# The product with the norm's weights at the end of the feed-forward layers, on GpSimd

## The chip, the cores and the metric

The program runs on one core of one Trainium2 chip. The metric is the device time of one execution in microseconds (us). The engines are PE (matmuls and transposes), VectorE (DVE in the rows), ScalarE (ACT), GpSimd (POOL) and SyncE (SP, whose queue starts most transfers). Each engine takes its instructions in a fixed order and waits at its head until what the instruction needs is there.

## What is computed

Two blocks, one after the other, on 512 rows of 1024 numbers. The first has two layers of attention and of a mixture of experts. The second has two layers, each with a feed-forward part, a mixer and a second feed-forward part. All four feed-forward parts end in the same way, and that ending is what the change touches:

```python
def rms_norm_2(x, gain):
    x32 = x.astype(jnp.float32)
    y = x32 * lax.rsqrt(jnp.mean(x32 * x32, axis=-1, keepdims=True) + RMS_EPS) * gain.astype(jnp.float32)
    return y.astype(x.dtype)

def swiglu(h, w_gate, w_up, w_down):
    return (jax.nn.silu(h @ w_gate) * (h @ w_up)) @ w_down

f = swiglu(rms_norm_2(h, g[0]), ffn_w_gate[layer, 0], ffn_w_up[layer, 0], ffn_w_down[layer, 0])
h = h + 0.5 * rms_norm_2(f, g[1])
hm = rms_norm_2(h, g[2])
```

So at the end of a feed-forward part each row of its result f is multiplied by the norm's weights (g[1], with the 0.5 in it) and by one number, the reciprocal root of its mean square, and added to h. The next stage begins with another such norm of the new h.

## The kernel before

The 512 rows are four tiles t of 128 rows; h lies in `X` and f in `F`, both 128 partitions by 4 tiles by 1024 columns, float32, in SBUF. A tile is worked on in two halves of 512 columns. Matmuls in float32 precision are made of three passes (`mm3`, lines 207 to 209): each operand is split into a rounded high part (ScalarE, line 202) and the rest (line 203, VectorE, now and then GpSimd).

`ffn` goes over the 2816 hidden columns in three groups c. For the last, c = 2, `tok_major` runs the last four weight rows tile by tile: 24 matmuls of 512 columns finish a tile, 12 for a half. Then, for tile t, `evac` adds the two banks to `F` (line 1113) and calls `post_add`:

- `rms(hs, "post")`: ScalarE squares each half and sums it up (line 1043; the tile named `junk` takes the squares, `ss` the sums), VectorE joins the two sums to `ms` (line 1045), GpSimd raises it to the power -0.5, `rr` (line 1047).
- line 1060 multiplies each half of `F` by the weights `gain`, in place.
- line 1062 adds `F` times `rr` to each half of `X`.
- `feed` (line 241 and 222) makes the norm for the next stage: the same four steps over `X`, `xn` as the normed tile on VectorE in two halves, four transposes on PE for each half, and the split of the transposed columns to `xt` (ScalarE line 202, VectorE line 203). PE needs `xt` of all four tiles for the next stage's first matmuls, or of tiles 0 and 1 for their first halves.

At the last feed-forward part there is no `feed`: each half of `X` is sent to the output.

The order on each engine is made by a scheduler from the code and a model of durations; `issue_after(after)` keeps line 1060, on the engine of the instruction named `after`, behind the tile's second addition (line 1113). It adds nothing for an instruction on another engine. Line 1060 has other callers too (the mixers' ends), which pass no `after`.

Of the kernel before, what the change touches and what calls it, by code (L numbers as in the profile page):

```python
# [14 lines left out]
OP = mybir.AluOpType  # L15
# [94 lines left out]
class Core:  # L110
# [942 lines left out]
    def post_add(self, t, hs, g, feed=True, after=None):  # L1053

        V = self.nc.vector
        r = self.rms(hs, "post")
        xs = self.halves(self.X[:, t, :])
        with self.tc.issue_after(after) if after else nullcontext():
            for h in range(2):
                V.tensor_tensor(hs[h], hs[h], g[:, h * 512:(h + 1) * 512], op=OP.mult)  # L1060
        for h in range(2):
            V.scalar_tensor_tensor(xs[h], hs[h], r, xs[h], op0=OP.mult, op1=OP.add)  # L1062
        if self.nxt and feed:
            self.feed(t)
        if not self.nxt:
            o = self.out[0, t * P:(t + 1) * P, :]
            for q, y, x in zip((self.nc.sync, self.nc.scalar), self.halves(o), xs):
                q.dma_start(y, x)
# [423 lines left out]
```

## Time and profile before

| | us |
|---|---|
| median of 3 runs | 2849.36 |
| lowest and highest | 2843.97, 2851.26 |
| the profiled execution | 2851.15 |
| its span in the profile | 2849.4 |

Busy in the profiled execution: PE 2754.2 us, VectorE 1525.3, ScalarE 1194.9, GpSimd 233.9. The clock granted to PE is at its full level in nearly all of the span (0.983 on average). A busy PE is one whose pipeline is not empty; what it loses is seen in the rows on whom it waited for. In the timeline a row's bracket is the idle time of the engine ahead of it, and what ended it.

The rows that the prediction rests on stand below, behind the change.

### The profile page before, as it was taken

To read this page: it belongs to the slowest core of one execution; us is meant where nothing else is said; L and a number is where in the kernel's file an instruction comes from. 1 tells how busy PE (TensorE), PEld (TensorE's weight loads), DVE (VectorE), ACT (ScalarE), POOL (GpSimd) and SP (SyncE) were. 2 spreads that over 40 slices of the span, in tenths; PEclk is the share of its full clock that TensorE was granted. 3 is DMA by queue.
4 is the path that set the end of the run, shared out by engine and by line. 5 is a ranking of instruction groups with operands and counts; after the bars stand their busy time and mean duration, and the time that the engine had idled before them with its cause. 6 is when DMAs were issued, how large, how long until landed. Compare 5 with 4: busy or idle time off the path is not lost.

```text
span 2849.4 us, 35986 instructions
## 1 busy us (share of the span) xinstructions
PE 2754.2 (97%) x14092; PEld 2278.2 (80%) x14092; DVE 1525.3 (54%) x2819; ACT 1194.9 (42%) x2141; POOL 233.9 (8%) x233
## 2 busy tenths in 40 slices
PE   8998999998999999999999999999999999999998
PEld 6766986766896888888888887998888787788886
DVE  7965987976896323356533237343233644632334
ACT  4374983375893222234423224232322445532222
POOL 0031211041211000010100001000000000100000
PEclk9999999999999999999999999999999999999999
DMA  4316976216995323314232333333232314133320
GB/s 168 79 41 223 341 290 215 60 35 219 318 342 186 107 89 104 104 57 136 92 100 89 103 103 109 133 122 104 89 104 89 111 39 141 53 105 103 97 92 33
DMA packets 180000, 365.07 MB, mean 128 GB/s; under 512 B 14544, under 2 KB 115152, under 8 KB 172272
## 3 DMA queue, kind: packets, MB, share of 16 engines
q1 hardware_dynamic: 169264, 336.35, 35.2%
q0 software_dynamic: 9984, 25.31, 2.6%
q8 instruction: 112, 1.84, 0.3%
q10 hardware_dynamic: 576, 1.05, 0.1%
q14 instruction: 64, 0.52, 0.1%
HBM read 343.73 MB, written 27.33 MB: 130 GB/s over the span
## 4 chain that ended last, share of the span: by engine, by line
PE 74%; DVE 6%; ACT 1%; issue 1%; POOL 1%; DMA 1%; POOLq 0%; DVEq 0%; ACTq 0%; SPq 0%
PE psa L209 19%; PE psa L207 19%; PE psa L208 19%; PE pst L209 3%; PE pst L207 3%; PE pst L208 3%; PE psa L1297 1%; PE pst L1325 1%; DVE xn L241 1%; DVE hl L203 1%; POOL rr L1047 1%; DVE X L1062 1%; PE pst L222 1%; PE pst L1315 0%; DVE xt L203 0%
## 5 line engine op out<-in xcount | busy, mean ns | idle before, releaser
L203 DVE TENSOR_TENSOR hl<-raw,hl 128x1024 fp32r<-128x1024 f32 (+2 forms) x451 | 552.3, 1231 | 778.6 <-ACT hl L202 777.6
L202 ACT CAST hl<-raw 128x1024 fp32r<-128x1024 f32 (+1 forms) x456 | 471.8, 1042 | 682.2 <-PE psa L209 327.9
L209 PE MATMUL psa<-xt,hl 128*128 128x512 f32 (+1 forms) x1632 | 602.7, 369 | 1.9 <-DVE hl L203 1.9
L207 PE MATMUL psa<-xt,hl 128*128 128x512 f32 (+1 forms) x1632 | 603.0, 370 | 0.7 <-ACT xt L202 0.7
L208 PE MATMUL psa<-xt,hl 128*128 128x512 f32 (+1 forms) x1632 | 603.0, 370 | 0.2 <-DVE xt L203 0.2
L209 PEld LDWEIGHTS psa<-xt,hl 128*128 128x128 f32 x1632 | 309.0, 189 | 53.2 <-DVE hl L203 2.3
L207 PEld LDWEIGHTS psa<-xt,hl 128*128 128x128 f32 x1632 | 309.0, 190 | 52.8 <-ACT xt L202 1.1
L208 PEld LDWEIGHTS psa<-xt,hl 128*128 128x128 f32 x1632 | 309.1, 189 | 51.8 <-DVE xt L203 0.6
L207 PE MATMUL psa<-hl,xt 128*128 128x512 f32 (+2 forms) x608 | 245.4, 405 | 3.5 <-ACT hl L202 3.5
L209 PE MATMUL psa<-hl,xt 128*128 128x512 f32 (+2 forms) x608 | 245.5, 404 | 0.0
L208 PE MATMUL psa<-hl,xt 128*128 128x512 f32 (+2 forms) x608 | 241.8, 398 | 3.2 <-DVE hl L203 3.0
L1098 ACT ACTIVATE silu<-psa 128x512 f32<-128x512 f32 x88 | 52.6, 597 | 345.7 <-PE psa L209 345.7
L207 PE MATMUL psa<-hl,hT 128*128 128x512 f32 (+1 forms) x480 | 189.0, 394 | 0.0
L209 PE MATMUL psa<-hl,hT 128*128 128x512 f32 (+1 forms) x480 | 187.8, 391 | 0.0
L208 PE MATMUL psa<-hl,hT 128*128 128x512 f32 (+1 forms) x480 | 187.8, 391 | 0.0
L1099 DVE TENSOR_TENSOR silu<-silu,psa 128x512 f32<-128x512 f32 x88 | 60.5, 687 | 217.5 <-PE psa L209 217.1
L1047 POOL TENSOR_TENSOR rr<-ms,consts 128x1 f32<-128x1 f32 x52 | 38.6, 744 | 1632.4 <-DVE ms L1045 1621.5
L207 PEld LDWEIGHTS psa<-hl,xt 128*128 128x128 f32 x608 | 139.2, 229 | 21.7 <-ACT hl L202 3.7
L208 PEld LDWEIGHTS psa<-hl,xt 128*128 128x128 f32 x608 | 139.6, 230 | 18.8 <-DVE hl L203 5.3
L209 PEld LDWEIGHTS psa<-hl,xt 128*128 128x128 f32 x608 | 139.3, 229 | 13.5 <-issue 1.0
L207 PE MATMUL psa<-hl,xgT 128*96 128x256 f32 x512 | 145.5, 284 | 0.5 <-ACT xgT L202 0.5
L208 PE MATMUL psa<-hl,xgT 128*96 128x256 f32 x512 | 143.1, 280 | 0.0
(366 smaller groups left out, 4419.2 us busy)
## 6 DMA issues: line engine op xcount, KB each, us to landing
raw<-in_ffn_w_gate_dram SPq DMA_DIRECT2D x44, 1024.0 KB
raw<-in_ffn_w_up_dram SPq DMA_DIRECT2D x44, 1024.0 KB
raw<-in_ffn_w_down_dram SPq DMA_DIRECT2D x44, 1024.0 KB
raw<-in_w_up_dram SPq DMA_DIRECT2D x16, 1024.0 KB
raw<-in_w_gate_dram SPq DMA_DIRECT2D x12, 1024.0 KB
raw<-in_w_down_dram SPq DMA_DIRECT2D x12, 1024.0 KB
xt<-in_w_down_dram SPq DMA_DIRECT2D x12, 1024.0 KB
xt<-in_w_gate_dram SPq DMA_DIRECT2D x10, 1024.0 KB
```

Of the source, the lines that this page charges most:

```text
L202: self.nc.scalar.copy(hi, src)
L203: return (self.nc.gpsimd if pool else self.nc.vector).tensor_tensor(lo, src, hi.bitcast(F32), op=OP.subtract)
L207: mm(out, lhs[0], rhs[0], start=start, stop=False)
L208: mm(out, lhs[0], rhs[1], start=False, stop=False)
L209: mm(out, lhs[1], rhs[0], start=False, stop=stop)
L222: self.nc.tensor.transpose(ps[:, k * P:(k + 1) * P], src[:, (4 * h + k) * P:(4 * h + k + 1) * P], self.ident)
L241: self.nc.vector.scalar_tensor_tensor(o, i, r, gh, op0=OP.mult, op1=OP.mult)
L1047: nc.gpsimd.tensor_tensor(r, ms, self.c("nhalf")[:, :1], op=OP.pow)
L1062: V.scalar_tensor_tensor(xs[h], hs[h], r, xs[h], op0=OP.mult, op1=OP.add)
L1098: A.activation(s, acc[0], AF.Silu)
L1099: V.tensor_tensor(s, s, acc[1], op=OP.mult)
L1297: PE.matmul(ps[:, (j - j0) * nk + b * P:(j - j0) * nk + (b + 1) * P], qT[half(par), j, :], kv["k", g, kb][half(par), j, :], start=True, st ...
```

## The change

One line of `post_add` is changed. Where `after` is given, which only the feed-forward parts do, the product of line 1060 is issued on GpSimd, else on VectorE as before. There are 4 parts, 4 tiles and 2 halves: 32 instructions of 128x512.

```diff
         with self.tc.issue_after(after) if after else nullcontext():
             for h in range(2):
-                V.tensor_tensor(hs[h], hs[h], g[:, h * 512:(h + 1) * 512], op=OP.mult)
+                (self.nc.gpsimd if after else V).tensor_tensor(hs[h], hs[h], g[:, h * 512:(h + 1) * 512], op=OP.mult)
```

Since the product writes the half that ScalarE's square reads, it waits for that square. The scheduler lays all engines' orders out anew around it.

GpSimd at the end of the first feed-forward part, before; the pairs of `rr` are those of `F` and of `X` of one tile, and `hl` is the rest of a weight split for the next stage:

```order
L1047 TENSOR_TENSOR rr_11585<-ms_11583,consts_72 128x1
L1047 TENSOR_TENSOR rr_11597<-ms_11595,consts_72 128x1
L1047 TENSOR_TENSOR rr_11648<-ms_11646,consts_72 128x1
L1047 TENSOR_TENSOR rr_11660<-ms_11658,consts_72 128x1
L1047 TENSOR_TENSOR rr_11711<-ms_11709,consts_72 128x1
L203 TENSOR_TENSOR hl_11831<-raw_11823,hl_11831 128x1024
L1047 TENSOR_TENSOR rr_11723<-ms_11721,consts_72 128x1
L1047 TENSOR_TENSOR rr_11774<-ms_11772,consts_72 128x1
L1047 TENSOR_TENSOR rr_11786<-ms_11784,consts_72 128x1
```

The same place in the change:

```order
L1060 TENSOR_TENSOR F_9482<-F_9482,gain_9479 128x512 x2
L1047 TENSOR_TENSOR rr_11585<-ms_11583,consts_72 128x1
L1047 TENSOR_TENSOR rr_11597<-ms_11595,consts_72 128x1
L1060 TENSOR_TENSOR F_9482<-F_9482,gain_9479 128x512 x2
L1047 TENSOR_TENSOR rr_11648<-ms_11646,consts_72 128x1
L1047 TENSOR_TENSOR rr_11660<-ms_11658,consts_72 128x1
L1060 TENSOR_TENSOR F_9482<-F_9482,gain_9479 128x512 x2
L1047 TENSOR_TENSOR rr_11711<-ms_11709,consts_72 128x1
L1060 TENSOR_TENSOR F_9482<-F_9482,gain_9479 128x512
L1047 TENSOR_TENSOR rr_11723<-ms_11721,consts_72 128x1
L203 TENSOR_TENSOR hl_11831<-raw_11823,hl_11831 128x1024
L1060 TENSOR_TENSOR F_9482<-F_9482,gain_9479 128x512
```

Both products of a tile stand ahead of its first `rr`, the next tile's behind its second; the last tile's first product stands ahead of tile 2's second `rr`, the other behind the weight split. At the ends of the second and third part the order is the same but for the split, which isn't there.

VectorE at the same end, from the additions of tile 0 on, before:

```order
L1113 TENSOR_TENSOR F_9482<-F_9482,psa_11478 128x512
L1113 TENSOR_TENSOR F_9482<-F_9482,pst_11482 128x512
L1060 TENSOR_TENSOR F_9482<-F_9482,gain_9479 128x512
L1045 TENSOR_SCALAR ms_11583<-ss2_11579 128x1
L1060 TENSOR_TENSOR F_9482<-F_9482,gain_9479 128x512
L1062 SCALAR_TENSOR_TENSOR X_6608<-F_9482,rr_11585,X_6608 128x512 x2
L1113 TENSOR_TENSOR F_9482<-F_9482,psa_11486 128x512
L1045 TENSOR_SCALAR ms_11595<-ss2_11591 128x1
L241 SCALAR_TENSOR_TENSOR xn_11599<-X_6608,rr_11597,gain_11471 128x512 x2
L1113 TENSOR_TENSOR F_9482<-F_9482,pst_11490 128x512
```

And in the change:

```order
L1113 TENSOR_TENSOR F_9482<-F_9482,psa_11478 128x512
L1113 TENSOR_TENSOR F_9482<-F_9482,pst_11482 128x512
L1045 TENSOR_SCALAR ms_11583<-ss2_11579 128x1
L1062 SCALAR_TENSOR_TENSOR X_6608<-F_9482,rr_11585,X_6608 128x512 x2
L1113 TENSOR_TENSOR F_9482<-F_9482,psa_11486 128x512
L1045 TENSOR_SCALAR ms_11595<-ss2_11591 128x1
L241 SCALAR_TENSOR_TENSOR xn_11599<-X_6608,rr_11597,gain_11471 128x512 x2
L1113 TENSOR_TENSOR F_9482<-F_9482,pst_11490 128x512
```

Only the products are gone here; the second addition of the next tile still stands behind both halves of `xn`.

PE at the transposes (line 222) of tile 1 of the same end, before; `psa` and `pst` are banks, and the lines 207 to 209 are matmuls of the last tile:

```order
L208 MATMUL psa_11502<-hl_11542,hT_11336 128x512
L209 MATMUL psa_11502<-hl_11542,hT_11336 128x512
L207 MATMUL psa_11502<-hl_11547,hT_11402 128x512
L222 MATMUL pst_11665<-consts_72,xn_11662 128x128 x4
L208 MATMUL psa_11502<-hl_11547,hT_11402 128x512
L222 MATMUL psa_11672<-consts_72,xn_11662 128x128 x4
L209 MATMUL psa_11502<-hl_11547,hT_11402 128x512
```

In the change:

```order
L208 MATMUL pst_11498<-hl_11550,hT_11464 128x512
L209 MATMUL pst_11498<-hl_11550,hT_11464 128x512
L207 MATMUL psa_11502<-hl_11539,hT_11274 128x512
L222 MATMUL pst_11665<-consts_72,xn_11662 128x128 x4
L222 MATMUL psa_11672<-consts_72,xn_11662 128x128 x4
L208 MATMUL psa_11502<-hl_11539,hT_11274 128x512
L209 MATMUL psa_11502<-hl_11539,hT_11274 128x512
```

Both groups stand earlier in the last tile's matmuls, and no matmul is left between them.

## Rows read from the trace of the kernel before

**Rows 1.** The page, part 1: busy us, share of the span, instructions
```profile
PE 2754.2 (97%) x14092; PEld 2278.2 (80%) x14092; DVE 1525.3 (54%) x2819; ACT 1194.9 (42%) x2141; POOL 233.9 (8%) x233
```

**Rows 2.** PE's waits at ends 1, 2, 3: us in total, times, longest
```profile
PE pst L222 <- DVE xn L241: 2.8, 3, 1.2
PE psa L209 <- DVE hl L203: 0.5, 1, 0.5
...
PE pst L222 <- DVE xn L241: 1.8, 3, 1.2
...
PE psa L208 <- DVE hl L203: 2.2, 1, 2.2
PE pst L222 <- DVE xn L241: 1.5, 2, 1.2
```

**Rows 3.** Timeline, end 1, tile 0: start, us, engine, line, instruction [idle before <-releaser]
```profile
1246.36 0.69 DVE L1113 TENSOR_TENSOR F<-F,pst 128x512 f32<-128x512 f32 x1 [2.03 <-PE pst L209]
...
1247.14 0.63 ACT L1043 ACTIVATE junk<-F 128x512 bf16<-128x512 f32 x1 [2.06 <-DVE F L1113]
...
1247.90 0.21 DVE L1045 TENSOR_SCALAR ms<-ss 128x1 f32<-128x1 f32 x1 [0.25 <-ACT junk L1043]
...
1248.03 0.68 DVE L1060 TENSOR_TENSOR F<-F,gain 128x512 f32<-128x512 f32 x1
1248.19 0.93 POOL L1047 TENSOR_TENSOR rr<-ms,consts 128x1 f32<-128x1 f32 x1 [338.79 <-DVE ms L1045]
...
1249.15 1.42 DVE L1062 SCALAR_TENSOR_TENSOR X<-F,rr,X 128x512 f32<-128x512 f32 x2 [0.44 <-POOL rr L1047]
...
1250.69 0.63 ACT L1043 ACTIVATE junk<-X 128x512 bf16<-128x512 f32 x1
...
1251.81 0.55 POOL L1047 TENSOR_TENSOR rr<-ms,consts 128x1 f32<-128x1 f32 x1 [2.69 <-DVE ms L1045]
...
1252.39 1.42 DVE L241 SCALAR_TENSOR_TENSOR xn<-X,rr,gain 128x512 f32<-128x512 f32 x2 [0.73 <-POOL rr L1047]
...
1253.20 0.66 PE L222 MATMUL pst<-consts,xn 128*128 128x128 f32 x4 [1.21 <-DVE xn L241]
```

**Rows 4.** Timeline of PE, end 1: transposes of tiles 0 to 2
```profile
1253.93 0.60 PE L222 MATMUL psa<-consts,xn 128*128 128x128 f32 x4
...
1260.99 0.66 PE L222 MATMUL pst<-consts,xn 128*128 128x128 f32 x4
1261.73 0.60 PE L222 MATMUL psa<-consts,xn 128*128 128x128 f32 x4
...
1271.54 0.66 PE L222 MATMUL pst<-consts,xn 128*128 128x128 f32 x4 [1.18 <-DVE xn L241]
```

**Rows 5.** Products on GpSimd (ns min/median/max; mean ns), weight cast on ScalarE
```profile
L587 POOL TENSOR_TENSOR X<-X,gb x6: 2362/2384/2408, 240.9 to 684.5; 128x1024 f32<-128x1024 f32 x6
...
L529 POOL TENSOR_TENSOR rows<-rows,den 128x512 f32<-128x512 f32 x8 | 8.2, 1038 | 110.9 <-DVE den L527 110.2 <-DVE m L516 0.7
...
L202 ACT CAST hl<-raw 128x1024 fp32r<-128x1024 f32 (+1 forms) x456 | 471.8, 1042 | 682.2 <-PE psa L209 327.9
```

**Rows 6.** Timeline: VectorE and GpSimd at the same time, near 1377 and 452 us
```profile
1377.29 3.52 DVE L241 SCALAR_TENSOR_TENSOR xn<-X,rr,gain 128x512 f32<-128x512 f32 x2
...
1377.73 2.53 POOL L203 TENSOR_TENSOR hl<-raw,hl 128x1024 fp32r<-128x1024 f32 x1
...
451.87 0.68 DVE L203 TENSOR_TENSOR xt<-psa,xt 128x512 fp32r<-128x512 f32 x1
...
451.43 2.36 POOL L587 TENSOR_TENSOR X<-X,gb 128x1024 f32<-128x1024 f32 x1 [3.07 <-DVE X L586]
```

**Rows 7.** Timeline, last end, tile 3
```profile
2838.67 0.19 ACT L1043 ACTIVATION_READ_ACCUMULATOR junk<-F 128x1 f32 x1
...
2839.24 0.86 POOL L1047 TENSOR_TENSOR rr<-ms,consts 128x1 f32<-128x1 f32 x1 [4.58 <-DVE ms L1045]
2840.14 1.42 DVE L1062 SCALAR_TENSOR_TENSOR X<-F,rr,X 128x512 f32<-128x512 f32 x2 [0.44 <-POOL rr L1047]
```

## The prediction

> **What bounds the kernel now.** I read the page's busy shares first: PE is busy 97% of the span, VectorE 54% [rows 1]. PE takes its instructions in a fixed order, so a wait of PE at its head goes into the time in full, and a microsecond saved on VectorE is worth something only where PE waits for VectorE. So next I read whom PE waits for around the three feed-forward ends that have a stage behind them (from 1236, 1726 and 2236 us; I call them ends 1, 2, 3), and the fourth end, at 2836 us, with which the program stops. At end 1 PE waits 2.8 us for `xn` and 0.5 for a weight split, at end 2 1.8 for `xn`, at end 3 1.5 for `xn` and 2.2 for a weight split, 8.8 us in all [rows 2]. That is the most that a faster ending could bring.
>
> Then I read one tile's chain from the timeline [rows 3], start to start. Second half of F added 1246.36, its square on ScalarE 1247.14 (0.78 later), `ms` 1247.90 (0.76), `rr` on GpSimd 1248.19, X updated 1249.15, second square of X 1250.69 (1.54), the next `rr` 1251.81 (1.12), `xn` 1252.39 (0.58), transposes on PE 1253.20 (0.81), for which PE has waited 1.21. VectorE's second product with the weights runs from 1248.03 inside the wait for `rr`; it only lengthens `rr` from 0.55 to 0.93.
>
> **What the change does to one tile.** It removes 32 products of 0.68 us from VectorE, eight at each end, and puts 32 on GpSimd. The product writes the half that the square reads, so it can't run beside that square; it starts when the square is done. In GpSimd's printed order both products of a tile stand ahead of that tile's `rr`, and behind the second `rr` of a tile stands the next tile's first product (two, where its squares are done).
>
> *Price of one product on GpSimd.* No row shows it. The same form at twice the width takes 2.36 to 2.41 us; a product with a broadcast operand at this width 1.04 [rows 5]. Half of 2.385 is 1.19, and I add 0.09 for the start-up, which doesn't halve: 1.28. The ends are 1.04 and 1.4; I stay by the first row, since the form is the same. The Trainium skill (GPSIMD Engine Reference, section 3.1, Elementwise) gives 4497 ns for 2048 columns with two inputs, which would be an estimate of 1.12 for this width; by it the sum below falls by about 3.5 us. No run here shows that figure.
>
> *First cost: the product is now ahead of `rr`.* Square's start to its end 0.73, hand-over 0.08, product 1.28, `rr` to X 0.58. The chain from the addition to the transposes is then 0.78 + 0.81 + 1.28 + 0.58 + 1.54 + 1.12 + 0.58 + 0.81 = 7.50 us, against 6.84 in the trace [rows 3].
>
> *Second cost: the two engines shut each other out.* At 1377 us a pair of `xn` took 3.52 us instead of 1.42, while GpSimd worked from 1377.73 to 1380.26 on a split with two SBUF inputs: the second half waited for it and was done 0.55 after it. A VectorE instruction with one operand in PSUM ran its usual 0.68 in the middle of a GpSimd product [rows 6]. Now GpSimd has a product queued directly behind the `rr` that releases `xn`, so it stands between the two halves of `xn`: the second half ends about 1.13 + 0.55 = 1.7 us after the first, not 0.67. The addition of the next tile is queued behind that half on VectorE, so the whole next chain starts later too.
>
> *Third cost: PE's order.* The transposes stand earlier among the matmuls than before: the first by one, the second tile's by five (24 matmuls between the first tile's and the second's, counted in the printed order, where there were 29), with its two groups back to back. Matmul slots are 0.23: 7.06 us between 1253.93 and 1260.99 for one group of transposes and 29 matmuls [rows 4].
>
> **The sum.** Waits of PE at end 1, group by group. Tile 0, first half: 1.21 + 0.64 (the longer chain) + 0.23 (one place earlier) = 2.1; second half 1.2 (1.7 less its own 0.35 and a matmul). Tile 1: the next chain starts 0.15 before the transposes of tile 0's second half, so 7.50 - 0.15 = 7.35 lies between them; PE has work for 7.06 - 5 x 0.23 = 5.9, so it waits 1.4, then 1.7 - 0.35 = 1.4 for the second half. Tile 2: three more things stand in that chain: a copy of 512 transposed columns ahead of the square (0.5, half of the cast of 1024), a weight cast of 1.04 between the squares of X [rows 5], and the last tile's first product ahead of `rr` (1.25): 10.2 us from group to group. Before, 9.81 lay between them [rows 4], of which 1.7 was waiting [rows 2, 4], so some 8.1 of work; 0.2 to 0.8 less now, and I take 7.7: a wait of 2.5. Its second half waits 2.3 at end 1, where a weight split is next on GpSimd, such a one as the 2.53 of rows 6. Tile 3 at end 1: GpSimd still has that split, the last product and `rr` to do, X follows some 5.3 us after tile 2's `xn`, and `xn` some 10.1 after it; PE, with 44 half-width matmuls in between, is there after 9.3: 1.6 and 0.6. Sum of end 1: 2.1 + 1.2 + 1.4 + 1.4 + 2.5 + 2.3 + 1.6 + 0.6 = 13.1. At ends 2 and 3 GpSimd has a product and no split behind tile 2's `rr` (1.2, not 2.3), and tile 3's transposes stand behind 29 full matmuls, so that 0.8 and 0.3 are left for it: 10.6 and 10.1. Walking the old order in the same way gave 1.2, 0.2, 0.8, 1.3 and 0.6 at end 1, where the trace has 1.21, none, 0.5, 1.18 and 0.4 (what is left of the 2.8) [rows 2 to 4], which is why I trust the steps to half a microsecond each.
>
> Less what is there now [rows 2]: 13.1 - 3.3 = 9.8, 10.6 - 1.8 = 8.8, 10.1 - 3.7 = 6.4; at end 3 the 2.2 for the weight split goes, because its cast and split come while PE stands at the transposes. Last end: there is no PE work behind it. The last square's total is read at 2838.67 for 0.19, the product 2838.94 to 2840.22, `rr` until 2840.75 and X at 2840.78 instead of 2840.14 [rows 7]: 0.6. The VectorE time removed, 32 x 0.6 = 19 us, I cost at nothing: it lay beside PE work or inside the wait for `rr`. Total +25.6, rounded to 25 since I allow half a microsecond for later small waits that the delay covers. The profiled execution took 2851.15 (span 2849.4), 1.8 above the median of three, 2849.36; I put the sum on the median: **2874 us**.
>
> **Rivals.**
> - *No shutting out at this width.* If the product and `xn` ran side by side, the second halves would not wait and tile 1 would start earlier; the first and third costs stay. The same walk gives 5.6, 3.7, 2.3 and 0.6: 2861.6; with a product of 1.04 us 2858. Against it speak the 3.52 and the 0.93 [rows 3, 6].
> - *GpSimd first.* `xn` starts 0.03 after `rr`'s end, and GpSimd's next instruction is ready at once. If it goes first, both halves of `xn` stand behind it: about 15.3, 11.7 and 11.0 of waits, less 8.8, plus 0.6: 2879. For it: the product needs no signal from another engine. Against it: at 1377.29 `xn`'s first half kept its length although GpSimd began in the middle of it [rows 6]. The Trainium skill (SBUF — State Buffer, Who interferes with whom) says that whichever issues first keeps the shared pair for the whole instruction; that leaves both orders open.
> - *Faster.* Around the ends VectorE, not PE, is the engine with the dense queue, and eight products less at each end free 4.8 us there. If `xn` of every tile came that much sooner, PE's 8.8 us of waiting would go: 2840.6. The Trainium skill (Perfetto Trace Analysis, Optimizing Scalar/DVE Operations) has it that offloading a saturated VectorE, even to GpSimd, may make sense, and adds that it might not help between these two. It decides at the product's price: only if GpSimd is done with it before `ms` reaches it, in some 0.3 us, is `rr` not later than now; the nearest row is 1.04 [rows 5], and the transposes' earlier places would eat the gain.
> - *Nothing to see.* The added waits could be given back if later stages had waits on the same engines to absorb them. Rows 2 leave 2.7 us of such waits (both for weight splits), so this needs most steps above to be wrong by half: about 2852.
>
> **How the numbers follow.** Forecast 0.72, no shutting out 0.10, GpSimd first 0.08, nothing to see 0.07, faster 0.03. The range takes in the two slower rivals and the product's price (1.04 takes 5 us off, 1.4 adds 2.5): 2860 to 2882. A measurement of this kernel tells some 0.3%, 8.5 us, from no change; slower by more than that has 0.90 (the first three), within it 0.07, faster 0.03.
>
> **What would show it.** Right: 32 products on GpSimd of 1.2 to 1.3 us undisturbed, some 1.8 where they start beside `xn`; pairs of `xn` of 2.5 us; PE's waits for `xn` at the three ends up from 6.1 to 30 us or more, with a wait before the second group of each pair; `rr` of 0.55 at the last end, X there 0.6 later. Wrong: `xn` pairs still 1.42 (no shutting out), first halves of `xn` of 1.9 (GpSimd first), or PE's waits for `xn` no longer than before.

## The result

The changed kernel took 2875.74 us (median of 4 runs, 2871.13 to 2880.66) against 2849.25 before: a ratio of 1.009, 95% interval 1.0078 to 1.0102. Five more runs beside the last experiments gave 2871.57 (1.0080, 1.0067 to 1.0093). It is slower by some 25 us, and the forecast of 2874 stands. Not all of its steps do. In the table of the experiments one run of the kernel with the first halves, of 9444.2 us where its ten others took 2850.65 to 2862.18, is left out.

The profiled execution took 2871.13 us. Its busy times (the page, part 1) answer to [rows 1]:

```profile
PE 2757.9 (96%) x14092; PEld 2281.5 (80%) x14092; DVE 1516.0 (53%) x2787; ACT 1194.3 (42%) x2141; POOL 270.8 (9%) x265
```

GpSimd has 36.9 us more, VectorE only 9.3 less, though 32 products of 0.68 (21.8 us) have left it: some of its other instructions became longer. The line's own summary (ns, min/median/max) says what a product costs:

```profile
L1060 POOL TENSOR_TENSOR F<-F,gain x32: 1261/1286/1714, 1243.5 to 2858.3; 128x512 f32<-128x512 f32 x32
```

PE's waits at ends 1, 2 and 3 (us, times, longest), which answer to [rows 2]:

```profile
PE pst L222 <- DVE xn L241: 8.4, 3, 4.6
...
PE pst L222 <- DVE xn L241: 8.3, 3, 3.1
...
PE pst L222 <- DVE xn L241: 7.1, 3, 3.1
```

Together 23.8 us where there were 8.8, and the 2.2 for a weight split at end 3 is gone. The timeline of end 1, tile 0, which answers to [rows 3], shows how; its last two rows are the first transposes of tiles 1 and 2:

```profile
1244.74 0.69 DVE L1113 TENSOR_TENSOR F<-F,pst 128x512 f32<-128x512 f32 x1 [2.03 <-PE pst L209]
...
1246.32 1.29 POOL L1060 TENSOR_TENSOR F<-F,gain 128x512 f32<-128x512 f32 x1 [1.49 <-ACT junk L1043]
1247.57 0.55 POOL L1047 TENSOR_TENSOR rr<-ms,consts 128x1 f32<-128x1 f32 x1
1248.15 1.42 DVE L1062 SCALAR_TENSOR_TENSOR X<-F,rr,X 128x512 f32<-128x512 f32 x2 [1.66 <-POOL rr L1047]
...
1250.81 0.55 POOL L1047 TENSOR_TENSOR rr<-ms,consts 128x1 f32<-128x1 f32 x1 [2.69 <-DVE ms L1045]
...
1251.33 1.26 POOL L1060 TENSOR_TENSOR F<-F,gain 128x512 f32<-128x512 f32 x1
1251.39 2.41 DVE L241 SCALAR_TENSOR_TENSOR xn<-X,rr,gain 128x512 f32<-128x512 f32 x2 [0.73 <-POOL rr L1047]
1253.19 0.94 PE L222 MATMUL pst<-consts,xn 128*128 128x128 f32 x4 [3.05 <-DVE xn L241]
...
1254.35 1.05 PE L222 MATMUL psa<-consts,xn 128*128 128x128 f32 x4
...
1262.35 0.66 PE L222 MATMUL pst<-consts,xn 128*128 128x128 f32 x4 [0.75 <-DVE xn L241]
...
1275.26 1.12 PE L222 MATMUL pst<-consts,xn 128*128 128x128 f32 x4 [4.57 <-DVE xn L241]
```

- *The chain.* From the second addition's start to X's start there are 3.41 us (1244.74 to 1248.15); before, 2.79 (1246.36 to 1249.15). The product stands ahead of `rr`: 0.62 us.
- *The collision.* The next tile's product starts at 1251.33, 0.06 ahead of `xn`, and `xn` takes 2.41 instead of 1.42. From its start to the transposes of its first half (1253.19) there are 1.80 us, where there were 0.81 [rows 3], and the transposes of the second half follow with no wait. Tile 1's `xn` stands behind a product in the same way (1260.52 and 1260.45), tile 2's behind the weight split (1272.38 and 1272.31; its first half takes 2.82).
- *The clock.* The transposes then take 0.94 and 1.05 where they took 0.66 and 0.60. The stretches (last but two column: the granted clock as a share of 2.4 GHz) after and before, 1250 to 1260 and 1270 to 1280 us:

```profile
1250.00:1260.00 10.00, 6.95 (x28) 5.75 (x28) 7.22 (x12) 4.73 (x14) 3.64 (x5) 0.83 0.00 2
1270.00:1280.00 10.00, 5.31 (x27) 4.81 (x27) 8.19 (x10) 5.49 (x12) 6.30 (x5) 0.70 0.45 157
...
1250.00:1260.00 10.00, 8.79 (x43) 7.07 (x42) 8.56 (x16) 5.85 (x16) 1.51 (x3) 1.00 0.01 2
1270.00:1280.00 10.00, 8.39 (x70) 7.90 (x69) 8.80 (x18) 3.51 (x8) 2.18 (x3) 1.00 0.64 186
```

Of the 20 us, PE was granted its lower level, 1.2 GHz, for about 9 ((0.17 + 0.30) x 10 us x 2), behind waits of 3.05 and 4.57 us. Before, there was none.

### The profile page after: what moved, and what is told of

Same layout as the page of the kernel before. It is cut to its first block, busy times and chain, and to the rows that moved or that the text cites. A ratio compares the mean times of both kernels' runs of the same rounds, so it can differ in the third digit from the quotient of the medians.

```text
span 2869.3 us, 35987 instructions
## 1 busy us (share of the span) xinstructions
PE 2757.9 (96%) x14092; PEld 2281.5 (80%) x14092; DVE 1516.0 (53%) x2787; ACT 1194.3 (42%) x2141; POOL 270.8 (9%) x265
## 3 DMA queue, kind: packets, MB, share of 16 engines
q10 hardware_dynamic: 576, 1.05, 0.1%
## 4 chain that ended last, share of the span: by engine, by line
PE 61%; DVE 4%; ACT 1%; POOL 1%; issue 1%; POOLq 0%; DVEq 0%; ACTq 0%
PE psa L207 16%; PE psa L209 16%; PE psa L208 16%; PE pst L207 3%; PE pst L209 3%; PE pst L208 3%; DVE xn L241 1%; PE psa L1297 1%; PE pst L1325 1%; ACT junk L1043 1%; POOL rr L1047 1%; DVE X L1062 1%; PE pst L222 1%; POOL F L1060 1%; PE pst L1315 0%
## 5 line engine op out<-in xcount | busy, mean ns | idle before, releaser
L1060 POOL TENSOR_TENSOR F<-F,gain 128x512 f32<-128x512 f32 x32 | 41.3, 1293 | 1402.0 <-ACT junk L1043 1402.0
```

The lines of the kernel that those rows point to most:

```text
L1060: (self.nc.gpsimd if after else V).tensor_tensor(hs[h], hs[h], g[:, h * 512:(h + 1) * 512], op=OP.mult)
```

## The experiments

**How the runs are compared.** A few microseconds are at stake, and the runs of one kernel differ by more. What they differ by is PE's granted clock: over 64 runs of the kernel before, its mean is 0.9834, and a straight line through time and clock gives 2.16 us less for each 0.001 more (2857.22 us is a run at 0.981, 2841.85 one at 0.987; the correlation is -0.93, and 1.1 us are left as scatter). With that slope the difference of the means is divided into a part for the clock and a rest; the rest is good to perhaps 1.5 us, since the clock is listed to 0.001. Beside it stands what the profile of the kernel shows: the waits at ends 1 to 3 (PE for `xn`, for a weight split, and in one kernel for ScalarE; before 8.8 us) less 8.8, plus what the last end became longer by (first addition there to the last X). The diffs show only what differs, from the change or from the run that the text names; some of their lines end at an open bracket.

| kernel | runs | median us | ratio, 95% interval | mean clock | less clock: rest | waits, less 8.8 | last end | sum |
|---|---|---|---|---|---|---|---|---|
| the change, all 9 runs | 9 | 2873.51 | 1.009 and 1.008 | 0.9804 | +24.5 - 6.4 = 18.2 | 15.0 | 2.2 | 17.2 |
| first halves only | 10 | 2856.4 | 1.003 (1.002 to 1.004) | 0.9836 | +7.1 + 0.5 = 7.5 | 8.0 | 0 | 8.0 |
| second halves only | 6 | 2864.66 | 1.0048 (1.0031 to 1.0065) | 0.9815 | +13.8 - 4.1 = 9.8 | 4.7 | 0.8 | 5.5 |
| zeros written instead | 11 | 2845.84 | 0.9989 (0.998 to 0.9997) | 0.9855 | -3.8 + 4.7 = 0.9 | 1.6 | 0 | 1.6 |
| last end only | 11 | 2852.45 | 1.0011 (1.0001 to 1.002) | 0.9828 | +2.7 - 1.2 = 1.4 | 0 | 2.2 | 2.2 |
| held behind `xn` | 6 | 2865.83 | 1.0055 (1.004 to 1.007) | 0.9812 | +16.3 - 4.8 = 11.5 | 10.2 | 2.2 | 12.4 |
| 0.1 us later | 6 | 2869.13 | 1.0065 (1.005 to 1.008) | 0.9823 | +18.9 - 2.3 = 16.7 | 12.3 | 2.2 | 14.5 |
| own tile, held | 12 | 2854.33 | 1.0013 (1.0004 to 1.0023) | 0.9840 | +4.5 + 1.3 = 5.8 | 7.8 | 0 | 7.8 |
| matmuls in the waits | 6 | 2881.38 | 1.0108 (1.009 to 1.0126) | 0.9817 | +31.6 - 3.7 = 27.9 | 14.5 + 13.2 | 2.2 | 29.9 |
| transposes later | 6 | 2870.27 | 1.0072 (1.0059 to 1.0085) | 0.9810 | +20.5 - 5.2 = 15.4 | 13.0 | 2.2 | 15.2 |
| own tile, held, later | 6 | 2858.3 | 1.0026 (1.0015 to 1.0038) | 0.9832 | +7.7 - 0.5 = 7.2 | 7.4 | 0 | 7.4 |
| before, transposes later | 11 | 2855.2 | 1.0016 (1.0007 to 1.0025) | 0.9815 | +5.1 - 4.2 = 0.9 | -1.0 | 0 | -1.0 |

(The 13.2 are the added matmuls themselves.) The rest and the sum agree within 2.2 us in all but the second halves (9.8 and 5.5; 1.6 of that are longer waits for `roped` in the stages behind). So the cost is PE's waits at the ends, and a clock part that differs from run to run.

**First halves only.** The product of h = 1 stays on VectorE.

```diff
-                (self.nc.gpsimd if after else V).tensor_tensor(
+                (self.nc.gpsimd if after and h == 0 else V).tensor_tensor(
```

> Only the first half's product goes to GpSimd; the second half's stays on VectorE. The product of the first half is ready some 0.8 us after the first addition, and before the second addition's square is done, so it is not in the chain ahead of rr. What is left is the collision with xn: the next tile's first product stands directly behind the rr that releases xn. Theory (the collision is the larger part of the cost): GpSimd goes first, xn pairs of 2.4 us instead of 1.42 at tiles 0 to 2, PE's waits for xn at ends 1 to 3 up from 6.1 to about 15, time 2857 to 2863. Rival (the longer chain is the cost, the collision is hidden): waits within 2 us of before's 6.1, time 2847 to 2851. At the last end no change (0).

2856.4 us. The product isn't in the chain here, and the timeline of tile 0 shows the collision alone:

```profile
1245.67 1.26 POOL L1060 TENSOR_TENSOR F<-F,gain 128x512 f32<-128x512 f32 x1
1245.73 2.40 DVE L241 SCALAR_TENSOR_TENSOR xn<-X,rr,gain 128x512 f32<-128x512 f32 x2 [0.73 <-POOL rr L1047]
```

PE's waits for `xn` came to 16.0. The theory put them at 15 and the time at 2857 to 2863: met, but for the last half microsecond. The collision is some 7.5 us.

**Second halves only.**

```diff
-                (self.nc.gpsimd if after else V).tensor_tensor(
+                (self.nc.gpsimd if after and h == 1 else V).tensor_tensor(
```

> Only the second half's product goes to GpSimd; the first half's stays on VectorE. The second half's product waits for the second square and stands ahead of rr, so the chain is 0.64 us longer, as in the full change. The next tile's second product can't start until its addition, which stands behind xn on VectorE, is done, so nothing collides with xn. Theory (collision the larger part): xn pairs 1.42, X 0.6 later per tile, PE's waits for xn at ends 1 to 3 up from 6.1 to about 11, time 2853 to 2858. Rival (the chain is the cost): nearly the whole of the full change's cost, 2865 or more.

2864.66 us, which is neither theory's 2853 to 2858 nor quite the rival's 2865 or more. Its clock was low (4.1 us); the rest, 9.8, is above the theory's 4 to 9. PE's waits for `xn` are 10.8, near the theory's 11. The chain is longer as expected (product 1245.11 to 1246.40, `rr` 1246.35), and tile 0's `xn` is back to 1.41:

```profile
1250.18 1.41 DVE L241 SCALAR_TENSOR_TENSOR xn<-X,rr,gain 128x512 f32<-128x512 f32 x2 [0.73 <-POOL rr L1047]
...
1252.90 0.68 DVE L1060 TENSOR_TENSOR F<-F,gain 128x512 f32<-128x512 f32 x1
...
1253.08 1.65 POOL L1060 TENSOR_TENSOR F<-F,gain 128x512 f32<-128x512 f32 x1 [2.94 <-ACT junk L1043]
```

What I had missed is in the last two rows: the first half's product on VectorE now runs into the second half's on GpSimd, both with two inputs in SBUF, and the latter takes 1.65 instead of 1.29, ahead of `rr`. The two halves' rests, 7.5 and 9.8, add up to 17.3, near the whole change's 18.2, though this second collision isn't in the whole change, and 2.7 of the 9.8 are seen in no wait. So both costs are real; which is the larger is not told.

**Zeros written instead.** GpSimd's instructions keep their place and their waits but read nothing.

```diff
+                [self.nc.gpsimd.memset(hs[h], 0.0) for _ in range(2)] if after else V.tensor_tensor(hs[h], hs[h], g[:, h * 512:(h + 1) * 512], op=OP.mult)
```

> Left out: the product with the weights; in its place GpSimd twice writes zeros into the half of F (so nothing of F reaches X at these ends). The waits on the square and by X are those of the full change, and so is the order on PE, but GpSimd's instructions read nothing from SBUF. If two such writes take about the product's 1.28 us: theory (GpSimd's reading shuts out xn, which reads two SBUF operands): xn pairs back to 1.42, PE's waits for xn at ends 1 to 3 some 3 us smaller at each end than in the full change, time 2858 to 2866. Rival (xn is late for another reason, the order on VectorE or PE): xn pairs still 2.4, time 2870 to 2878.

```profile
L1060 POOL MEMSET F<- x64: 518/527/531, 1245.9 to 2836.9; 128x512 f32 x64
...
1252.86 1.11 POOL L1060 MEMSET F<- 128x512 f32 x2
1252.94 1.41 DVE L241 SCALAR_TENSOR_TENSOR xn<-X,rr,gain 128x512 f32<-128x512 f32 x2 [0.67 <-POOL rr L1047]
```

2845.84 us, below the theory's 2858 to 2866 and below before. Two things follow, and one doesn't. The writes run beside `xn`, and `xn` keeps its 1.41: it is GpSimd's reading that shuts it out. (The Trainium skill, SBUF — State Buffer, Who interferes with whom, says just this: a VectorE instruction with two inputs in SBUF contends with a GpSimd instruction that reads SBUF, not with one that only writes it; the trace agrees, 1.41 against 2.41.) And VectorE's time: all 32 products are off it here, and the rest is 0.9, so taking them off brought no gain on balance, as costed. What doesn't follow is a price for the chain: one of the two writes (0.53 each) went behind `rr` in GpSimd's order, so the chain here was no longer than before. That is why the theory's time was missed.

**Last end only.**

```diff
-                (self.nc.gpsimd if after else V).tensor_tensor(
+                (self.nc.gpsimd if after and not self.nxt else V).tensor_tensor(
```

> The products go to GpSimd at the last feed-forward end alone; the first three ends are as before. The prediction gave this end 0.6 us. Theory now: two products (2.5), rr, X and the next tile's additions behind X on VectorE, and the squares form a loop longer than PE's 24 matmuls for a tile, so each of the last three tiles adds half a microsecond: distance between the rr of tiles 5.98 us instead of 5.44, X of the last tile about 2.1 us later than before after the last matmul; time 2850 to 2853. Rival (0.6 as predicted): distance 5.44, time 2849 to 2851. The two times can't be told apart by the median; the profile's distances tell.

2852.45 us. The times don't decide, as said; GpSimd's timeline does:

```profile
2824.11 0.55 POOL L1047 TENSOR_TENSOR rr<-ms,consts 128x1 f32<-128x1 f32 x1
2827.60 2.54 POOL L1060 TENSOR_TENSOR F<-F,gain 128x512 f32<-128x512 f32 x2 [2.94 <-ACT junk L1043]
2830.10 0.55 POOL L1047 TENSOR_TENSOR rr<-ms,consts 128x1 f32<-128x1 f32 x1
...
2836.08 0.57 POOL L1047 TENSOR_TENSOR rr<-ms,consts 128x1 f32<-128x1 f32 x1
...
2842.04 0.55 POOL L1047 TENSOR_TENSOR rr<-ms,consts 128x1 f32<-128x1 f32 x1
```

The `rr` are 5.96 to 5.99 us apart, before 5.44 (2822.93 to 2828.37 and on), which is PE's 24 matmuls. X of a tile waits for `rr`, the next tile's additions stand behind X on VectorE, its squares behind them, and both products behind these: that loop has become longer than PE's. From the first addition to the last X there are 24.06 us instead of 21.83: 2.2, where the prediction had 0.6.

**Held behind `xn`.** Three writes of zeros, into a half of F that is used up, stand on GpSimd between the `rr` that releases `xn` and the next tile's products.

```diff
+            if hold is not None:
+                with self.tc.issue_after(self.rr):
+                    for n in [512, 512, 512]:
+                        self.pad = self.nc.gpsimd.memset(hold[:, :n], 0.0).ins
...
+                with self.tc.issue_after(self.pad) if after and self.pad else nullcontext():
+                    (self.nc.gpsimd if after else V).tensor_tensor(hs[h], hs[h], g[:, h * 512:(h + 1) * 512], op=OP.mult)
```

> The full change, but on GpSimd three writes of zeros (128x512 each, 0.53 us in the run before this one; they read nothing, and go into a half of F that is already used up) stand behind the rr that releases xn, ahead of the next tile's products. So xn has its two halves done before a product starts, and the first product, which is not in the chain, only comes 1.6 us later. Theory (the collision with xn costs about 8 us of the whole): xn pairs of 1.42 us instead of 2.41 at tiles 0 and 1, PE's waits for xn at ends 1 to 3 from 24 down to about 15, time 2864 to 2870. Rival (GpSimd's products are now late for the next rr, or the collision was hidden): 2873 or more.

2865.83 us, and 16.0 of waits for `xn`, as the theory has it. In its timeline (the lines have moved: 1053 is `rr`, 247 `xn`):

```profile
1250.49 1.41 DVE L247 SCALAR_TENSOR_TENSOR xn<-X,rr,gain 128x512 f32<-128x512 f32 x2 [0.73 <-POOL rr L1053]
1258.41 1.41 DVE L247 SCALAR_TENSOR_TENSOR xn<-X,rr,gain 128x512 f32<-128x512 f32 x2 [0.66 <-POOL rr L1053]
```

The rest fell from 18.2 to 11.5: the collision again, 6.7 by its removal where the first halves alone gave 7.5.

**0.1 us later.** The same with one write of 128x1, to see whether `xn` goes first if it starts first.

```diff
-                    for n in [512, 512, 512]:
+                    for n in [1]:
```

> As the run with three writes of zeros, but with a single write of 128x1 (0.10 us): the next tile's product reaches GpSimd's head about 0.1 us after the rr that releases xn, and xn starts 0.03 to 0.06 us after that rr. Theory (who starts first keeps the other out for its whole instruction; in the full change GpSimd was ahead by 0.06 us): now the first half of xn goes at its usual 0.7, the product next, and the second half behind it; the pair still takes about 2.4 to 2.5, PE's wait moves from the first group of transposes to the second. Time within 3 us of the full change, 2872 to 2879. Rival (GpSimd always has precedence): first halves of xn of 1.7 or more, as in the full change.

```profile
1246.75 0.10 POOL L244 MEMSET F<- 128x1 f32 x1
1246.80 1.26 POOL L1067 TENSOR_TENSOR F<-F,gain 128x512 f32<-128x512 f32 x1
1246.83 2.44 DVE L247 SCALAR_TENSOR_TENSOR xn<-X,rr,gain 128x512 f32<-128x512 f32 x2 [0.72 <-POOL F L244]
...
1742.56 2.44 DVE L247 SCALAR_TENSOR_TENSOR xn<-X,rr,gain 128x512 f32<-128x512 f32 x2 [0.66 <-POOL F L244]
1742.61 1.85 POOL L1067 TENSOR_TENSOR F<-F,gain 128x512 f32<-128x512 f32 x1
...
1745.06 0.66 PE L222 MATMUL psa<-consts,xn 128*128 128x128 f32 x4 [0.62 <-DVE xn L247]
```

The write took less of the lead than I had counted on: at tile 0 of end 1 the product still starts 0.03 ahead, and `xn` again stands behind it. So it is at eight of the nine tiles. At the ninth, tile 1 of end 2, `xn` starts 0.05 ahead. There its first half takes its usual 0.75, the product takes 1.85 instead of 1.26, the second half stands behind the product, and PE waits 0.62 for that second half. So the one that starts first keeps the other out, as the theory has it; GpSimd has no standing precedence. It is one tile, but it is the order of the theory in every step. 2869.13 us is 3 below the expected range, most of which is the clock (0.9823; the rest is 16.7).

**Own tile, held.** The product writes a tile of its own (the memory of `silu`, free by then), so it doesn't wait for the square, and the three writes hold it behind `xn`.

```diff
+                q = self.fp.tile([P, 512], F32, name="silu", tag="silu", bufs=2) if after else hs[h]
+                qs.append(q)
-                    (self.nc.gpsimd if after else V).tensor_tensor(hs[h], hs[h], g[:, h * 512:(h + 1) * 512], op=OP.mult)
+                    (self.nc.gpsimd if after else V).tensor_tensor(q, hs[h], g[:, h * 512:(h + 1) * 512], op=OP.mult)
...
-            V.scalar_tensor_tensor(xs[h], hs[h], r, xs[h], op0=OP.mult, op1=OP.add)
+            V.scalar_tensor_tensor(xs[h], qs[h], r, xs[h], op0=OP.mult, op1=OP.add)
```

> The full change with two things taken away: the product writes a tile of its own instead of F, so it need not wait for ScalarE's square, and the three writes of zeros hold the next tile's products until xn is done. The second product then starts right behind the second addition, 0.8 us earlier, and is done about 0.3 us after ms is ready, while rr takes 0.55 instead of 0.93 because VectorE has no product beside it. Theory (these two are the whole cost of the change, and the time taken off VectorE is worth nothing): 2846 to 2852. Rival (something else of GpSimd's work costs, PE's order or the clock): 2856 or more. Second rival (VectorE's relief is worth something once the costs are gone): 2843 or less.

2854.33 us: between the theory's range and the first rival's. The rest is 5.8, so not waiting for the square took another 5.7 off (2.2 of them at the last end), and 5.8 stay. The timeline of PE and the others at tile 1 (1125 is the addition, 1071 the product, 1051 `ms`, 1053 `rr`) offered a cause:

```profile
1250.77 0.66 PE L222 MATMUL pst<-consts,xn 128*128 128x128 f32 x4 [1.54 <-DVE xn L247]
1251.18 0.48 PE L209 MATMUL pst<-hl,hT 128*128 128x512 f32 x1
...
1251.53 2.55 POOL L1071 TENSOR_TENSOR silu<-F,gain 128x512 f32<-128x512 f32 x2
1251.69 0.69 DVE L1125 TENSOR_TENSOR F<-F,pst 128x512 f32<-128x512 f32 x1 [0.32 <-PE pst L209]
...
1253.50 0.20 DVE L1051 TENSOR_SCALAR ms<-ss 128x1 f32<-128x1 f32 x1
...
1254.04 0.55 POOL L1053 TENSOR_TENSOR rr<-ms,consts 128x1 f32<-128x1 f32 x1
```

The scheduler had put tile 0's transposes one matmul ahead of the end of tile 1's own, so that PE, waiting for tile 0's `xn`, kept tile 1's second addition waiting too. The products also still hold up `rr`: it starts 0.54 us after `ms`, where there were 0.29 before [rows 3].

**Matmuls in the waits.** Ten bf16 matmuls of 128x512 on the square's output, ahead of the first transposes of tiles 0 and 2, to keep PE busy while it waits.

```diff
+            for _ in range(fill if h == 0 else 0):
+                self.nc.tensor.matmul(ps, self.junk[:, :P], self.junk, start=True, stop=True)
```

> The full change, and PE does ten matmuls of 128x512 more (bf16, on ScalarE's junk, into the bank that the transposes overwrite; about 2.3 us) ahead of the first transposes of tiles 0 and 2 at ends 1 to 3, where it waits 3 to 4.6 us; they can start as soon as the second square of X is done, some 3 us before xn. Nothing is left out. Theory (PE's long waits are followed by stretches at the lower of its two clock levels, and this is a third of the whole cost): no such stretches at end 1, granted clock of the runs up from 0.979 to about 0.983, time 2866 to 2871. Rival (the level has other causes, and the waits alone are the cost): clock unchanged, time 2874 to 2880.

2881.38 us, slower still and above both ranges; the mean clock was 0.9817 (the change's nine runs: 0.9804), and two stretches at the lower level were left at end 1. The scheduler put the added matmuls, and the transposes with them, 4 matmuls ahead of the end of tile 1's, and the next tile's `xn` (line 243) came 11.0 us after the first (1253.08 and 1264.10), where the change has 9.1 (1251.39 and 1260.52). Both the order and the work changed, so this doesn't tell whether the waits bring the lower level.

**The change again.** No edit.

> The full change once more, beside the next three on the same chip. Theory (about 8 us of its cost are a lower granted clock, which the added waits bring): mean granted clock of the runs 0.978 to 0.981, time 2872 to 2879. Rival (the first four runs happened to fall on a low clock; the waits alone cost some 18 us): mean clock 0.982 to 0.984, time 2865 to 2871.

2871.57 us with a mean clock of 0.9814: between the two times, and between the two clocks. Taken with the first four (0.9792) the clock's part is 6.4 of 24.5 us. It isn't tied to one place: this profile has 10.2 us of waits for `xn` at end 1, where the first had 8.4 and more of the lower clock. Its transposes of tiles 0 and 1 there:

```profile
1252.90 0.66 PE L222 MATMUL pst<-consts,xn 128*128 128x128 f32 x4 [3.05 <-DVE xn L241]
...
1261.88 0.66 PE L222 MATMUL pst<-consts,xn 128*128 128x128 f32 x4 [2.17 <-DVE xn L241]
```

Behind the same wait of 3.05 us tile 0's transposes ran at the full level here, and PE was sooner at tile 1's, so that it waited 2.17 for them where it had waited 0.75.

**Transposes later.** The full change, with tile 0's transposes behind the 7th matmul of tile 2 and tile 1's behind the 7th of tile 3.

```diff
+                        if self.late and n == at and t >= back:
+                            for i in done[t - back]:
+                                self.tc.add_manual_dep(i, self.mm.name, mybir.DependencyInfo(mybir.DependencyClass.NoSync, mybir.DependencyReason.DATA), reason="order")
```

> The full change with PE's transposes put later: those of tile 0 behind the 7th matmul of tile 2 instead of ahead of its first, those of tile 1 behind the 7th of tile 3 instead of its first; nothing else is ordered by hand. Theory (the earlier places cost what the prediction's third term says, 0.2 us for tile 0 and 1.15 for tile 1 at each of ends 1 to 3, some 4 us): 2868 to 2873 by the first four runs of the full change, or 3 to 6 us below what the run again gives. Rival (the tiles' own chain sets the pace, and PE waits for tile 2 and 3 what it no longer waits for tile 0): within 2 us of the full change.

2870.27 us, 1.3 below the change beside it, with intervals that overlap (the rest is 2.8 lower, and PE's waits are 2.0 shorter). The time lies in the theory's 2868 to 2873, the difference from the change beside it in the rival's "within 2 us", so the run doesn't tell them apart.

**Own tile, held, later.** The same edit in the kernel that gave 2854.

> The product in a tile of its own and held behind xn (the run that gave 2854), and PE's transposes put later as in the run before this one. In that run PE's transposes of tile 0 stood one matmul ahead of the end of tile 1's own matmuls, so tile 1's second addition, and its chain, waited for tile 0's xn. Theory (this order is all that was left of the cost): PE's waits for xn at ends 1 to 3 from 16.6 down to 8 or less, time 2842 to 2849. Rival (GpSimd's products are late for the next tile whatever PE does): waits of 14 or more, time 2851 to 2856.

2858.3 us, with waits for `xn` of 13.6 (16.2 with those for weight splits): near the rival's, and its time is passed by 2. So PE's order alone doesn't take away what was left. The timeline of tile 1 shows what came instead (1137 is the addition, 1083 the product, 1065 `rr`, 1063 `ms`, 1085 the two halves of X):

```profile
1252.53 1.70 POOL L247 MEMSET F<- 128x512 f32 x3
...
1253.94 0.68 DVE L1137 TENSOR_TENSOR F<-F,pst 128x512 f32<-128x512 f32 x1
...
1254.19 2.55 POOL L1083 TENSOR_TENSOR silu<-F,gain 128x512 f32<-128x512 f32 x2
...
1255.48 0.21 DVE L1063 TENSOR_SCALAR ms<-ss 128x1 f32<-128x1 f32 x1 [0.85 <-ACT junk L1061]
...
1256.69 0.56 POOL L1065 TENSOR_TENSOR rr<-ms,consts 128x1 f32<-128x1 f32 x1
...
1257.28 0.75 DVE L1085 SCALAR_TENSOR_TENSOR X<-silu,rr,X 128x512 f32<-128x512 f32 x1 [1.59 <-POOL rr L1065]
...
1259.15 0.74 DVE L1085 SCALAR_TENSOR_TENSOR X<-silu,rr,X 128x512 f32<-128x512 f32 x1
```

PE no longer keeps the addition waiting (1253.94, right behind `xn`), yet `rr` starts 1.21 us after `ms`, where there were 0.29 before [rows 3]. Held until `xn` is done, GpSimd has 2.55 us of products to do, and `ms` starts 1.3 us after they begin (2.0 in the run with the own tile held). Between one tile's `xn` and the next tile's `rr` there is no room for two products of this length: done earlier they shut out `xn`, done later they hold up `rr`. But that isn't all here: the scheduler also put both splits of `xt` on VectorE between the halves of X, so that the second half starts 1.87 us after the first, some 1.2 later than right behind it. With two things changed at once, this run doesn't tell how much of the 5.8 us that were left comes from PE's order and how much from `rr`.

**Before, transposes later.** The same edit in the kernel before, as the control.

> The kernel before, with PE's transposes put later in the same way and nothing else: the control for the two runs before this one. PE waited 1.2 us for tile 0's xn at each of ends 1 to 3 there. Theory (order alone is worth at most those waits): 2845 to 2849, 1 to 4 us less than before. Rival (later tiles' xn are the limit): 2849 to 2852.

2855.2 us, above both ranges, with a clock part of 4.2 and a rest of 0.9: no gain, as the rival says. One place from which the clock part can come is the stretch from 2414 to 2434 us, much the same place in the program (this kernel is 2.7 us ahead there); before, and then this kernel:

```profile
2414.00:2434.00 20.00, 16.34 (x97) 13.24 (x96) 11.23 (x49) 11.89 (x35) 0.00 (x0) 0.83 0.05 16
...
2414.00:2434.00 20.00, 17.51 (x74) 14.65 (x75) 8.02 (x33) 7.62 (x17) 0.00 (x0) 0.50 0.00 0
```

In this profile PE was at 1.2 GHz for the whole of it, before for a third. From the transposes of `rows` ahead of it to the first matmul on `full` there were 18.74 us before (2413.77 to 2432.51), and 24.00 in this kernel (2411.07 to 2435.07): 5.3 us longer. The profiles of the second halves and of the own tile have 0.51 in that stretch too. It lies in a stage that none of these edits touches.

None of the complete kernels beats the one before.

## Why the prediction was right, and where it wasn't

- **What bounds.** Right. PE's waits at three places in the program, and the loop of the last end, account for the time: 15.0 + 2.2 = 17.2 against a rest of 18.2. And nothing came back on balance from VectorE's relief (the zeros: 0.9).
- **The product's price.** 1.28 taken, 1.286 measured. The Trainium skill's figure (GPSIMD Engine Reference, section 3.1, Elementwise), an estimate of 1.12, is too low for this form.
- **First cost.** 0.64 taken (its own chain, 7.50 less 6.84, gives 0.66), 0.62 measured. In time it is a third to a half of the whole: 5.7 on its removal, 9.8 for the second halves alone, where another collision is in it.
- **Second cost.** That the engines shut each other out at this width was right, and the pair's length too (2.5 taken, 2.41 measured). The order was wrong: not between the halves of `xn` but ahead of both. The two engines were both free when `rr` ended, and the engine that made `rr` had its next instruction at its head: 0.06 us decided, as the run with 0.1 us shows by the one tile at which `xn` was ahead. The failed step is the one that took the row of 1377 us [rows 6], where `xn` had begun first, as the order here. So the rival "GpSimd first" named the mechanism, and its sign, first halves of `xn` of 1.9, came true (1.8); its waits of 15.3, 11.7 and 11.0 were too long.
- **The waits by tile, end 1.** Taken 3.3, 2.8, 4.8 and 2.2; measured 3.05, 0.75, 4.57 and none. From a tile's second addition to its transposes there are 8.45 us at tile 0 and 8.63 at tile 1 (1253.72 to 1262.35), where 7.50 were taken; 0.99 of it is the first half of `xn` behind the product. In the first profile no second half waits at any tile, as that order has it. PE came later to the transposes than taken, and so waited less: at 1.2 GHz for 9 of the 20 us around them, it took up to 4.5 us longer over its own work; in the second profile, with the full level at tile 0, tile 1's wait was 2.17. Waits and lost clock are up to 13 us together, where 13.1 of waits were taken. At end 2, without that in the first profile, 8.3 were measured and 10.6 taken, at end 3 7.1 and 10.1: the terms for tile 1's second wait and for tile 3 were too large. (By the terms that the prediction gives, ends 2 and 3 add up to 10.9 each; its sum would be 26.7.)
- **Third cost.** 0.2 and 1.15 us at each end, some 4 in all; the run with the transposes later gave 1.3 (medians) to 2.8 (rests), not told from nothing, and not from the 4 either.
- **Last end.** 0.6 taken, 2.2 measured. The chain of one tile was right; that VectorE's order makes the four chains a loop was overlooked, though the order printed ahead of the prediction for end 1 shows the additions behind X.
- **The clock.** Not in the prediction at all: 6.4 of 24.5 us.
- **Its signs.** Products of 1.2 to 1.3 us, pairs of 2.5 and `rr` of 0.55 came true. Waits for `xn` of 30 us or more (23.8), a wait before each second group (none in the first profile), products of 1.8 beside `xn` (1.26 to 1.29 where the product was first, 1.71 at most) and X 0.6 later at the last end (2.2) did not.

So the sum, 25, is right by luck, because two errors cancel: waits too long by 10 (25.0 net taken, 15.0 measured), against 6.4 of clock, 1.6 at the last end and what the rest holds beyond both. The mechanism was right but for the order of the two engines, the loop of the last end and the clock.

## What to carry to other kernels

An engine's spare time isn't the measure of a move; the gap on that engine between two things that wait for it is. Here GpSimd was 8% busy, but between one tile's `xn` and the next tile's `rr` it had some 1.3 to 2.0 us, and the two products need 2.55. Before a step is moved to GpSimd, look which VectorE instruction with two SBUF inputs is released by GpSimd's own last result: here the queued one went ahead of it, and shut it out for its whole length.

## What the runs showed of the hardware

- Two engines released by the same result: GpSimd's queued product began 0.06 us ahead of VectorE's `xn`, and 0.03 ahead even with a write of 0.10 us in between. Where `xn` began first, by 0.05 us at one tile, it kept its length (0.75 for the first half), and the product took 1.85 instead of 1.26. So the order of the starts decides.
- GpSimd's writes without a read (128x512, 0.53 us) leave a VectorE instruction with two SBUF inputs at its 1.41 for the pair.
- The granted clock of one and the same kernel runs from 0.981 to 0.987 over its runs, and 2.16 us go with each 0.001. One stretch of 20 us was at 0.83 in one profile and at 0.50 in another, with no change to its stage. The lower level came behind PE's long waits, though not behind all: of the twelve waits of 3.05 us or more in the two profiles of the change, nine were followed by transposes at the lower level (0.73 to 1.12 us for a group), three by transposes at the full one (0.66); the eight waits for `xn` in the profile before, of 0.28 to 1.23 us, were all followed by the full level. How much of the 6.4 us of clock the change brings stays open: the kernels with more waiting tend to the lower clocks (0.9804 for the change, 0.9855 for the zeros), but the control with no more waiting than before had 0.9815.
